# Writing VectorE's order over the output projection and twenty steps of the input projection, with weight sums a chunk sooner and results added by accumulating stores

## The chip, the cores and the metric

One core of a Trainium2 chip runs the whole program. The metric is device time in microseconds (us), the median of several executions; lower is better. "Chunk", "panel" and "step" are explained below.

## What is computed

One residual block on 512 tokens of width 2048, everything in float32 (cut to what matters; RMS norms, rotary angles and gains are left out):

```
h = rms_norm(x)
proj = h @ w_in                       # 2048 -> 15424 columns, split into 13 parts
o_conv = (b_gate * conv3(c_gate * u) * silu(conv_z)) @ w_conv_out
o_mla  = (attention(c_q, c_kv, k_rope) * silu(mla_z)) @ w_mla_out
o_mem  = (attention(mem_q, mem) * silu(mem_z)) @ w_mem_out
merged = sigmoid(g_conv)*o_conv + sigmoid(g_mla)*o_mla + sigmoid(g_mem)*o_mem
out = x + merged @ w_o
```

The change touches the first product (`w_in`) and the last line (`w_o`, and the sum with `x`).

## The kernel before

**Three products for one.** A float32 matrix is split into a high part and a low remainder, and a product is made as high*high + high*low + low*high, three TensorE matmuls (`mm3`, L161 to L163). The third is the first to read the low part of the weights. So for each piece of weights ScalarE writes the high part (`whi`, L281) and then VectorE the low part (`wlo`, L282).

**Panels and chunks.** `w_in`, `w_mla_out` and `w_o` go through a Strassen-like scheme: seven products in place of eight. A *panel* is 256 output columns and takes four *chunks* of weights, each 512 KB. A chunk is 42 matmuls (two blocks of rows, seven products, three matmuls). Before its split a chunk needs three *sums* on VectorE (L276, L277, L278), which fill the extra blocks of its `raw` tile. When a panel's last chunk is done, ScalarE copies one block out of PSUM (L317) and VectorE makes the panel's results in five instructions (L318, L323, L324, L326, L327), called the *eviction* here. The input projection has 60 panels, the output projection 8. Both begin with this order of chunks: three of panel 0, three of panel 1, then the last of panel 0 and the last of panel 1; after that panel by panel. In the texts c0, c1, ... are the chunks of the input projection and k0 to k31 those of the output projection, in this order; a *step* is one chunk.

**What prepares a chunk.** `queue` holds one entry for each chunk, and `begin(at, stage)` brings the entry at place `at` to a stage: 1 issues its load (SP's queue), 2 makes its sums, 3 its split. `take()` (L183) is called once a chunk, before TensorE's 42 matmuls: it splits this chunk (if need be) and the next, makes the sums of the one after that, issues the load of the third, runs one entry of the list `fills`, and pops the queue. There are four `raw` buffers, and two each for `whi` and `wlo`: ScalarE can write `whi` of chunk n+1 only when TensorE has finished chunk n-1.

**Who sets the order.** SP's and TensorE's instructions run in the order in which the code is written. For the other engines a scheduler picks the order, except inside `manual_dve`, where VectorE's is the written one too. In the kernel before, that stretch covers the end of the memory-key projection and the first 6 steps of the input projection (L821), and, later, the last product before the output projection and its first 9 steps (L1367 ff.).

**Other work of VectorE at these two places.** At the start of the input projection the last two of eight blocks of `x` are prepared through `fills`: a scaling and sums (L497, L255, L256, L258), then a split (L262). The first eight panels (`finish`) are kept as high and low parts: ScalarE squares them (L635, TensorE then adds the squares up, L641) and writes the high parts, VectorE the low ones (L134), and a store to DRAM goes through POOL. At the start of the output projection the last `merged` blocks get their sums (`sums_out`, L255 to L258, three instructions) and their split (`split_out`, L261 on ScalarE, L262 on VectorE), again through `fills`. Each panel of the output projection but the last is added to a block of `x` by VectorE (`result`, two instructions at L1350; the block `xr` was loaded by SP) and stored by ScalarE's queue. The last panel has a short way of its own (`tail_o`).

Of the kernel before, what the change touches and what calls it, by code (L numbers as in the profile page):

```python
# [30 lines left out]
P = 128  # L31
S = 512
# [75 lines left out]
def body(ctx, tc, a, out):  # L108
# [65 lines left out]
    def begin(at, stage):  # L174

        if at < len(queue):
            entry = queue[at]
            if len(entry) == 1:
                entry.append(entry[0]())
            while len(entry) < 2 + stage:  # L180
                entry.append(next(entry[1]))

    def take(ahead=1):  # L183
        for at in range(1 + ahead):
            begin(at, 3)
        begin(1 + ahead, 2)
        begin(2 + ahead, 1)
        if fills:
            fills.pop(0)()
        return queue.pop(0)[4]  # L190
# [332 lines left out]
    def staged_parts():  # L523
# [3 lines left out]
    upcoming(*plain_jobs([a["w_mem_kv"][grp][c] for grp in range(4) for c in range(8)], 512, True,  # L527
                         (staged_parts, None, None),
                         lambda c: memory_load(c + 1) if c < 4 else None))
    work = panels(xp, a["w_h"], len(SEQUENCE), lambda n: make(n), lambda n, e: finish(n, e), "aux")  # L530
    queue.insert(32 + 15, [lambda: rotary_weights()])
    parts_of_x = all_parts()
    manual_dve = ExitStack()
# [48 lines left out]
                nc.scalar.dma_start(mvdram[2 * (grp - 2) + i], t)  # L582
    for _ in parts_of_x:
        pass
    begin(2, 2)
    close_st()
    close_mt()
    pxb, close_xb = open_pool("xb", "right")
# [170 lines left out]

    conv_e = {}  # L760

    def make(n):
        return etile(), None

    angles = rotary()
# [50 lines left out]
    for i in (6, 7):  # L816
# [1 line left out]
        x_load(i, etile())  # L818
        steps = x_pair(i)
        fills += [lambda steps=steps: (next(steps), next(steps)), lambda steps=steps: next(steps)]  # L820
    for _ in range(6):  # L821
        next(work)
    manual_dve.close()
    for _ in work:
        pass
# [466 lines left out]
    def split_out(n):  # L1292
# [8 lines left out]
                 17: ((split_out, 1), (merged, 2), (merged, 3), (gate_load, 5), (gate_load, 6)),  # L1301
                 22: ((sums_out, 2),), 23: ((split_out, 2),), 24: ((sums_out, 3),),
                 25: ((split_out, 3), (merged, 4), (merged, 5), (gate_load, 7)),
                 29: ((sums_out, 4),), 30: ((split_out, 4), (merged, 6)), 31: ((sums_out, 5),),
                 32: ((split_out, 5),)}

    late_blocks = []
    for k in (6, 7):
# [6 lines left out]
    for tag, width in (("acc", 512), ("aux", 512), ("acc", 512), ("aux", 256), ("aux", 256)):  # L1315
        if done == 7:
            work = panels(xp, a["w_o"], 8, lambda n: make_o(n), lambda n, e: finish_o(n, e),
                          tail=lambda b, e: tail_o(b, e))
        banks = [bank(tag) for _ in range(width // P)]
        for n in dense_units(banks, width, actm, "F"):  # L1320
            if done == 0 and n == 8:
                for k in (6, 7):
                    nc.sync.dma_start(r32(late_blocks[k - 6]), amdram[k])
            if n % 4 == 3:
                step += 1
                for do, k in steps_out.get(step, ()):
                    do(k)
        for i in range(width // 256):
            gated(done + i, banks[2 * i:2 * i + 2])
        done += width // 256  # L1330
# [6 lines left out]

    def make_o(n):
        def middle():
            xrs[n] = pe.tile([P, 2, S], F32, tag="xr", name="xr", bufs=2)  # L1340
            nc.sync.dma_start(xrs[n].rearrange("p f n -> p (f n)"), a["xT"][:, n])
        return pe.tile([P, 8, H], F32, tag="e", name="e", bufs=2), middle

    def finish_o(n, e):
        fills.append(lambda: result(n, e))

    def result(n, e):
        xr = xrs[n]
        for f in range(2):
            vec.tensor_tensor(out=xr[:, f], in0=two(e)[:, f], in1=xr[:, f], op=ALU.add)  # L1350
            nc.scalar.dma_start(out[(2 * n + f) * P:(2 * n + f + 1) * P], xr[:, f])

    def tail_o(b, e):

# [10 lines left out]
        nc.sync.dma_start(out[15 * P:16 * P], xr[:, 1])  # L1365

    merged(7)  # L1367
    fills += [lambda: None, lambda: sums_out(6), lambda: split_out(6), lambda: sums_out(7), lambda: split_out(7)]
    for n, _ in enumerate(work):
        if n == 8:  # L1370
            manual_dve.close()
    close_e()
    close_m()
    close_x()
# [76 lines left out]
```

## Time and profile before

| | |
|---|---|
| median of 3 runs | 2164.0 us (2162.38 to 2164.59) |
| the profiled execution | 2162.43 us, of which its span is 2160.7 us |
| TensorE busy in the span | 2122.6 us (98%) |
| VectorE / ScalarE busy | 1728.2 us (80%) / 1010.8 us (47%) |
| input projection | about 107 to 1175 us of the span |
| output projection | about 1984 to 2157 us of the span |

In the timeline a row is: start, duration (both us), engine, line, operation, output<-inputs, shape, count, and in brackets the idle time before it with what ended it. Instructions of VectorE overlap a little, so the distance from one start to the next is what a place in its queue costs. Matmuls overlap too: one shows about 0.28 us, but they follow each other in 0.12 us. In the windows view a row is: the stretch, its length, then busy time and count of instructions of TensorE, its weight loads, VectorE, ScalarE and POOL, the granted TensorE clock (1.00 is full), the busy share of the DMA engines, and GB/s.

### The profile page before, as it was taken

How to read it: one execution, taken by the hardware profiler on the slowest of the kernel's cores; microseconds unless marked ns; L12 is line 12 of the kernel's file. 1: busy time of each engine (PE TensorE's matmuls, PEld its weight loads, DVE VectorE, ACT ScalarE, POOL GpSimd, SP SyncE). 2: the span in 40 equal slices, each digit the busy share in tenths (PEclk: the TensorE clock that was granted, in tenths of full speed). 3: DMA queues.
4: the chain of work that ended last, by engine and by line, in shares of the span. 5: the costliest groups of instructions: out<-in, count | busy, mean ns of one | idle time of the engine just before them, and what ended most of it. 6: DMA issues, size and time to landing. Idle time of an engine off the chain costs nothing.

```text
span 2160.7 us, 38707 instructions
## 1 busy us (share of the span) xinstructions
PE 2122.6 (98%) x16040; PEld 2037.7 (94%) x16040; DVE 1728.2 (80%) x2740; ACT 1010.8 (47%) x1235; POOL 130.9 (6%) x189
## 2 busy tenths in 40 slices
PE   9989999999999999999999999999999999999899
PEld 7889999999999999999999999898988899987899
DVE  5986878888888888888878876788886688856886
ACT  6743444444444344344444444777765533323333
POOL 0000000000000000000000000212111100011000
PEclk9999999999999999999999999999999999999999
DMA  8634443333333333343444336222346957667443
GB/s 330 248 98 137 158 135 128 128 127 128 127 127 127 125 125 126 126 136 133 137 137 142 131 129 241 90 104 81 112 158 245 355 203 208 201 213 199 141 162 107
DMA packets 93441, 338.51 MB, mean 157 GB/s; under 512 B 10896, under 2 KB 11152, under 8 KB 91216
## 3 DMA queue, kind: packets, MB, share of 16 engines
q1 hardware_dynamic: 70848, 252.58, 34.5%
q0 software_dynamic: 13920, 59.51, 8.6%
q10 hardware_dynamic: 8496, 23.94, 3.1%
q8 instruction: 125, 2.05, 0.4%
q14 instruction: 52, 0.43, 0.1%
HBM read 273.34 MB, written 62.65 MB: 156 GB/s over the span
## 4 chain that ended last, share of the span: by engine, by line
PE 84%; DVE 5%; ACT 2%; DMA 2%; issue 1%; POOL 0%; DVEq 0%; ACTq 0%; POOLq 0%
PE acc L161 14%; PE acc L163 14%; PE acc L162 14%; PE aux L161 13%; PE aux L163 13%; PE aux L162 13%; DVE wlo L282 2%; PE aux L363 1%; PE aux L997 1%; DMA raw<-in_w_h 1%; ACT whi L281 1%; DVE raw L276 0%; PE aux L977 0%; PE aux L980 0%; PE aux L978 0%
## 5 line engine op out<-in xcount | busy, mean ns | idle before, releaser
L281 ACT ACTIVATE whi<-raw 128x1792 fp32r<-128x1792 f32 x304 | 517.6, 1703 | 795.6 <-PE aux L162 336.7
L282 DVE TENSOR_TENSOR wlo<-raw,whi 128x1792 fp32r<-128x1792 f32 x304 | 614.8, 2022 | 204.2 <-ACT whi L281 203.5
L163 PE MATMUL aux<-xp,wlo 128*128 128x256 f32 (+1 forms) x1712 | 479.8, 280 | 6.3 <-DVE wlo L282 6.2
L161 PE MATMUL aux<-xp,whi 128*128 128x256 f32 (+1 forms) x1712 | 480.4, 281 | 0.0
L162 PE MATMUL aux<-xp,whi 128*128 128x256 f32 (+1 forms) x1712 | 479.2, 280 | 0.0
L163 PE MATMUL acc<-xp,wlo 128*128 128x256 f32 x1680 | 470.2, 280 | 3.4 <-DVE wlo L282 3.4
L161 PE MATMUL acc<-xp,whi 128*128 128x256 f32 x1680 | 470.8, 280 | 0.0
L162 PE MATMUL acc<-xp,whi 128*128 128x256 f32 x1680 | 469.6, 280 | 0.0
L163 PEld LDWEIGHTS aux<-xp,wlo 128*128 128x128 f32 (+1 forms) x1712 | 321.1, 188 | 7.5 <-DVE wlo L282 7.5
L161 PEld LDWEIGHTS aux<-xp,whi 128*128 128x128 f32 (+1 forms) x1712 | 320.6, 187 | 0.0
L163 PEld LDWEIGHTS acc<-xp,wlo 128*128 128x128 f32 x1680 | 316.0, 188 | 4.6 <-DVE wlo L282 4.6
L162 PEld LDWEIGHTS aux<-xp,whi 128*128 128x128 f32 (+1 forms) x1712 | 320.2, 187 | 0.0
L161 PEld LDWEIGHTS acc<-xp,whi 128*128 128x128 f32 x1680 | 315.6, 188 | 0.0
L162 PEld LDWEIGHTS acc<-xp,whi 128*128 128x128 f32 x1680 | 315.1, 188 | 0.0
L276 DVE TENSOR_TENSOR raw<-raw 128x512 f32<-128x512 f32 x304 | 208.3, 685 | 36.5 <-DMA raw<-in_w_h 31.8
L155 DVE TENSOR_TENSOR wlo<-raw,whi 128x1024 fp32r<-128x1024 f32 (+2 forms) x89 | 100.5, 1131 | 75.1 <-ACT whi L154 72.7
L154 ACT ACTIVATE whi<-raw 128x1024 fp32r<-128x1024 f32 (+2 forms) x89 | 87.7, 986 | 101.4 <-PE acc L162 43.3
L278 DVE TENSOR_TENSOR raw<-raw 128x256 f32<-128x256 f32 x304 | 127.9, 422 | 6.3
L277 DVE TENSOR_TENSOR raw<-raw 128x256 f32<-128x256 f32 x304 | 127.9, 422 | 5.7
L161 PE MATMUL acc<-whi,blk 128*128 128x384 f32 (+1 forms) x224 | 84.2, 376 | 0.0
L356 POOL TENSOR_TENSOR rs_r<-rs_t,mhalf 128x2 f32<-128x2 f32 (+2 forms) x71 | 65.2, 929 | 276.7 <-DVE rs_t L355 217.2
L163 PE MATMUL acc<-whi,blk 128*128 128x384 f32 (+1 forms) x224 | 80.9, 361 | 0.0
(360 smaller groups left out, 3896.7 us busy)
## 6 DMA issues: line engine op xcount, KB each, us to landing
raw<-in_w_h SPq DMA_DIRECT2D x240, 512.0 KB, 3.5
raw<-in_w_mla_out SPq DMA_DIRECT2D x32, 512.0 KB, 4.2
raw<-in_w_o SPq DMA_DIRECT2D x32, 512.0 KB, 3.6
raw<-in_w_mem_kv SPq DMA_DIRECT2D x31, 512.0 KB, 7.4
gdram<-e ACTq DMA_DIRECT2D x22, 512.0 KB, 2.9
raw<-in_w_ukv SPq DMA_DIRECT2D x16, 512.0 KB, 4.3
raw<-in_w_conv_out SPq DMA_DIRECT2D x16, 512.0 KB, 8.3
aadram<-z POOLq DMA_DIRECT2D x8, 896.0 KB, 3.9
```

The source lines that it names most:

```text
L154: act.activation(hi[:, cols], raw[:, cols], AF.Copy)
L155: vec.tensor_tensor(out=lo[:, cols], in0=raw[:, cols], in1=r32(hi[:, cols]), op=ALU.subtract)
L161: nc.tensor.matmul(o, lhsT=s[0], rhs=m[0], start=start, stop=False, skip_group_check=shared)
L162: nc.tensor.matmul(o, lhsT=s[0], rhs=m[1], start=False, stop=False, skip_group_check=shared)
L163: nc.tensor.matmul(o, lhsT=s[1], rhs=m[0], start=False, stop=stop, skip_group_check=shared)
L276: vec.tensor_tensor(out=f[:, 4:6], in0=f[:, 1:3], in1=f[:, 0:1].to_broadcast([P, 2, 256]), op=ALU.add)
L277: vec.tensor_tensor(out=f[:, 6], in0=f[:, 5], in1=f[:, 1], op=ALU.add)
L278: vec.tensor_tensor(out=f[:, 7], in0=f[:, 6], in1=f[:, 3], op=ALU.add)
L281: act.activation(hi, f[:, 1:8], AF.Copy)
L282: vec.tensor_tensor(out=lo, in0=f[:, 1:8], in1=r32(hi), op=ALU.subtract)
L356: pool.tensor_tensor(out=r, in0=t, in1=mhalf[:, :n], op=ALU.pow)
L363: nc.tensor.transpose(out=b[:, i * P:(i + 1) * P], in_=s, identity=ident)
```

## The change

1. **Sums a chunk sooner.** While the list `deeper` holds an entry, `take()` brings two chunks beyond the split ones to stage 2, and loads the one after. It is on from step 6 to step 19 of the input projection, and through all of the output projection.
2. **VectorE's order written.** The written stretch of the input projection grows from 6 steps to 20; that of the output projection now runs to its end.
3. **Results of the first five panels of the input projection** are finished one step later, through `fills`. At the end of the memory part the sums of c2 are no longer made ahead (`begin(2, 2)` became `begin(2, 1)`), and in the output projection the split of `merged` block 5 moved one place later.
4. **Results added by stores.** In panels 12 to 18 of the input projection SP issues seven copies of 512 KB from `xT` straight to `out` (DRAM to DRAM). In the output projection a panel's result is added to `out` by one accumulating store from POOL's queue. VectorE's 14 additions (L1350), the seven loads of `xr` and the 14 stores on ScalarE's queue are gone. The last panel stays as it was.

Core of the diff:

```diff
     def take(ahead=1):
         for at in range(1 + ahead):
             begin(at, 3)
-        begin(1 + ahead, 2)
-        begin(2 + ahead, 1)
+        more = 1 + ahead + len(deeper)
+        for at in range(1 + ahead, 1 + more):
+            begin(at, 2)
+        begin(1 + more, 1)
...
-    work = panels(xp, a["w_h"], len(SEQUENCE), lambda n: make(n), lambda n, e: finish(n, e), "aux")
+    work = panels(xp, a["w_h"], len(SEQUENCE), lambda n: make(n),
+                  lambda n, e: fills.append(lambda: finish(n, e)) if n < 5 else finish(n, e), "aux")
...
-    begin(2, 2)
+    begin(2, 1)
...
+    def out_rows(n):
+        return out[2 * n * P:2 * (n + 1) * P].rearrange("(f p) n -> p f n", f=2)
     def make(n):
+        if n >= 12 and n < 19:
+            nc.sync.dma_start(out_rows(n - 12), a["xT"][:, n - 12].rearrange("p (f n) -> p f n", f=2))
         return etile(), None
...
-    for _ in range(6):
+    for n in range(20):
+        if n == 6:
+            deeper.append(1)
         next(work)
+    deeper.clear()
     manual_dve.close()
...
     def finish_o(n, e):
-        fills.append(lambda: result(n, e))
-    def result(n, e):
-        xr = xrs[n]
-        for f in range(2):
-            vec.tensor_tensor(out=xr[:, f], in0=two(e)[:, f], in1=xr[:, f], op=ALU.add)
-            nc.scalar.dma_start(out[(2 * n + f) * P:(2 * n + f + 1) * P], xr[:, f])
+        nc.gpsimd.dma_start(out_rows(n), two(e), accum_op=ALU.add)
```

**Three places in VectorE's order.** Line numbers of the changed kernel are 4 or 5 higher for the same helper (L276 is L281, L282 is L287). First, the input projection from the split of the last block of `x` on. Before, c5 is `raw_1146`, c6 `raw_1208` and c8 `raw_1312`:

```order
L262 TENSOR_TENSOR xp7_1024<-e_1025,xp7_1024 128x1792
L276 TENSOR_TENSOR raw_1312<-raw_1312 128x512
L282 TENSOR_TENSOR wlo_1255<-raw_1146,whi_1254 128x1792
L276 TENSOR_TENSOR raw_1208<-raw_1208 128x512
L277 TENSOR_TENSOR raw_1312<-raw_1312 128x256
L277 TENSOR_TENSOR raw_1208<-raw_1208 128x256
L278 TENSOR_TENSOR raw_1312<-raw_1312 128x256
L278 TENSOR_TENSOR raw_1208<-raw_1208 128x256
L276 TENSOR_TENSOR raw_1364<-raw_1364 128x512
L277 TENSOR_TENSOR raw_1364<-raw_1364 128x256
L282 TENSOR_TENSOR wlo_1306<-raw_1208,whi_1305 128x1792
```

The same place after the change, with the same numbers for c5 and c6, and c7 as `raw_1261`:

```order
L267 TENSOR_TENSOR xp7_1021<-e_1022,xp7_1021 128x1792
L287 TENSOR_TENSOR wlo_1255<-raw_1146,whi_1254 128x1792
L281 TENSOR_TENSOR raw_1208<-raw_1208 128x512
L282 TENSOR_TENSOR raw_1208<-raw_1208 128x256
L283 TENSOR_TENSOR raw_1208<-raw_1208 128x256
L287 TENSOR_TENSOR wlo_1306<-raw_1208,whi_1305 128x1792
L281 TENSOR_TENSOR raw_1261<-raw_1261 128x512
```

Before, the sums of c8 and the first sums of c9 (`raw_1364`) stand ahead of the split of c6; now only c6's own sums stand between the splits of c5 and c6.

Second, a little later, from the split of c7 on. Before (c7 is `raw_1261`, c8 `raw_1312`):

```order
L282 TENSOR_TENSOR wlo_1358<-raw_1261,whi_1357 128x1792
L318 TENSOR_TENSOR e_1027<-aux_1029,e_1027 128x2x256
L278 TENSOR_TENSOR raw_1428<-raw_1428 128x256
L282 TENSOR_TENSOR wlo_1422<-raw_1312,whi_1421 128x1792
L323 TENSOR_TENSOR e_1027<-aux_1030,e_1027 128x512
```

After (c7 is `raw_1261`, c8 `raw_1312`, c9 `raw_1363`):

```order
L287 TENSOR_TENSOR wlo_1357<-raw_1261,whi_1356 128x1792
L281 TENSOR_TENSOR raw_1312<-raw_1312 128x512
L282 TENSOR_TENSOR raw_1312<-raw_1312 128x256
L283 TENSOR_TENSOR raw_1312<-raw_1312 128x256
L281 TENSOR_TENSOR raw_1363<-raw_1363 128x512
L282 TENSOR_TENSOR raw_1363<-raw_1363 128x256
L283 TENSOR_TENSOR raw_1363<-raw_1363 128x256
L323 TENSOR_TENSOR e_1024<-aux_1026,e_1024 128x2x256
L328 TENSOR_TENSOR e_1024<-aux_1027,e_1024 128x512
L329 SCALAR_TENSOR_TENSOR e_1024<-aux_1027,e_1024 128x256
L331 TENSOR_TENSOR e_1024<-aux_1028,e_1024 128x256
L332 TENSOR_TENSOR e_1024<-aux_1028,e_1024 128x256
```

The split of c8 follows directly on that. Before, it stood after the first instruction of panel 0's eviction; now two chunks' sums and the whole eviction stand between the splits of c7 and c8.

Third, the output projection from the split of k8 on. Before (k8 is `raw_22162`, k9 `raw_22213`, k11 `raw_22336`):

```order
L282 TENSOR_TENSOR wlo_22264<-raw_22162,whi_22263 128x1792
L276 TENSOR_TENSOR raw_22213<-raw_22213 128x512
L277 TENSOR_TENSOR raw_22336<-raw_22336 128x256
L277 TENSOR_TENSOR raw_22213<-raw_22213 128x256
L278 TENSOR_TENSOR raw_22336<-raw_22336 128x256
L278 TENSOR_TENSOR raw_22213<-raw_22213 128x256
L1350 TENSOR_TENSOR xr_21930<-e_21874,xr_21930 128x512 x2
L318 TENSOR_TENSOR e_22040<-aux_22042,e_22040 128x2x256
L323 TENSOR_TENSOR e_22040<-aux_22043,e_22040 128x512
L324 SCALAR_TENSOR_TENSOR e_22040<-aux_22043,e_22040 128x256
L326 TENSOR_TENSOR e_22040<-aux_22044,e_22040 128x256
L327 TENSOR_TENSOR e_22040<-aux_22044,e_22040 128x256
```

After (k8 is `raw_22116`, k9 `raw_22170`, k10 `raw_22221`):

```order
L287 TENSOR_TENSOR wlo_22273<-raw_22116,whi_22272 128x1792
L281 TENSOR_TENSOR raw_22221<-raw_22221 128x512
L282 TENSOR_TENSOR raw_22221<-raw_22221 128x256
L283 TENSOR_TENSOR raw_22221<-raw_22221 128x256
L323 TENSOR_TENSOR e_22050<-aux_22052,e_22050 128x2x256
L328 TENSOR_TENSOR e_22050<-aux_22053,e_22050 128x512
L329 SCALAR_TENSOR_TENSOR e_22050<-aux_22053,e_22050 128x256
L331 TENSOR_TENSOR e_22050<-aux_22054,e_22050 128x256
L332 TENSOR_TENSOR e_22050<-aux_22054,e_22050 128x256
L287 TENSOR_TENSOR wlo_22336<-raw_22170,whi_22335 128x1792
```

Before, the sums of k9 and k11 and the additions L1350 of panel 0 stand ahead of panel 1's eviction, and the split of k9 comes after it; now k9's sums are older, and between the splits of k8 and k9 stand only k10's sums and the eviction.

More of the change, by code (lines that the diff above doesn't have):

```diff
@@ L181, in begin @@
                 entry.append(next(entry[1]))
+    deeper = []
     def take(ahead=1):
@@ L1303, in body @@
                  25: ((split_out, 3), (merged, 4), (merged, 5), (gate_load, 7)),
-                 29: ((sums_out, 4),), 30: ((split_out, 4), (merged, 6)), 31: ((sums_out, 5),),
-                 32: ((split_out, 5),)}
+                 29: ((sums_out, 4),), 30: ((split_out, 4), (merged, 6)), 31: ((sums_out, 5),)}
     late_blocks = []
@@ L1318, in body @@
                           tail=lambda b, e: tail_o(b, e))
+            deeper.append(1)
         banks = [bank(tag) for _ in range(width // P)]
@@ L1339, in middle @@
         def middle():
-            xrs[n] = pe.tile([P, 2, S], F32, tag="xr", name="xr", bufs=2)
-            nc.sync.dma_start(xrs[n].rearrange("p f n -> p (f n)"), a["xT"][:, n])
+            if n == 7:
+                xrs[n] = pe.tile([P, 2, S], F32, tag="xr", name="xr", bufs=1)
+                nc.sync.dma_start(xrs[n].rearrange("p f n -> p (f n)"), a["xT"][:, n])
         return pe.tile([P, 8, H], F32, tag="e", name="e", bufs=2), middle
     def finish_o(n, e):
-        fills.append(lambda: result(n, e))
-    def result(n, e):
-        xr = xrs[n]
-        for f in range(2):
-            vec.tensor_tensor(out=xr[:, f], in0=two(e)[:, f], in1=xr[:, f], op=ALU.add)
-            nc.scalar.dma_start(out[(2 * n + f) * P:(2 * n + f + 1) * P], xr[:, f])
+        nc.gpsimd.dma_start(out_rows(n), two(e), accum_op=ALU.add)
     def tail_o(b, e):
@@ L1367, in body @@
     merged(7)
[L1368 to L1371, printed above, removed]
+    fills += [lambda: split_out(5), lambda: sums_out(6), lambda: split_out(6), lambda: sums_out(7), lambda: split_out(7)]
+    for _ in work:
+        pass
+    manual_dve.close()
     close_e()
```

## The prediction

> **What bounds the kernel now.** I read the engines' busy times first, then the windows view stage by stage, then the timeline of TensorE and of VectorE where TensorE loses time.
>
> ```profile
> PE 2122.6 (98%) x16040; PEld 2037.7 (94%) x16040; DVE 1728.2 (80%) x2740; ACT 1010.8 (47%) x1235; POOL 130.9 (6%) x189
> ```
>
> TensorE is the bound: it has 38 us of idle time in 2160.7. So this change can only win what TensorE loses in the two stages that it touches. The windows:
>
> ```profile
> 480.00:700.00 220.00, 220.00 (x1871) 220.00 (x1870) 187.15 (x254) 88.29 (x67) 1.60 (x3) 1.00 0.38 125
> ...
> 107.00:172.00 65.00, 55.17 (x453) 53.60 (x453) 57.35 (x77) 30.22 (x27) 0.73 (x1) 1.00 0.36 114
> ...
> 1984.00:2052.00 68.00, 57.10 (x461) 54.86 (x462) 60.18 (x78) 24.09 (x17) 1.41 (x2) 1.00 0.45 146
> 2052.00:2150.00 98.00, 98.00 (x835) 98.00 (x834) 80.57 (x108) 35.98 (x25) 0.00 (x0) 1.00 0.43 145
> ```
>
> In the middle of the input projection TensorE never rests: 220.00/1871 x 42 = 4.94 us a chunk. It idles in the first 65 us of that projection and the first 68 us of the output projection; from 2052 on it is full again. The rest of the kernel keeps its order. The first matmul that needs a chunk's low weights (L163) shows each chunk's delay:
>
> ```profile
> 107.12 0.39 PE L163 MATMUL aux<-xp,wlo 128*128 128x256 f32 x1
> ...
> 145.61 0.38 PE L163 MATMUL aux<-xp,wlo 128*128 128x256 f32 x1 [3.01 <-DVE wlo L282]
> ...
> 162.27 0.28 PE L163 MATMUL aux<-xp,wlo 128*128 128x256 f32 x1
> ...
> 166.98 1.84 PE L641 MATMUL acc<-one,e 128*128 128x1 f32 x16
> 169.76 1.95 PE L641 MATMUL acc<-one,e 128*128 128x1 f32 x16 [0.94 <-ACT e L635]
> ...
> 172.04 0.42 PE L163 MATMUL aux<-xp,wlo 128*128 128x256 f32 x1
> ```
>
> These are c0, c6, c9, two groups that add up squares, and c10. From c0 to c9 pass 55.15 us where nine chunks need 44.4: 10.7 us lost, all to late low weights. The 0.94 us ahead of the second group make 11.6.
>
> ```profile
> 1986.16 0.39 PE L163 MATMUL acc<-xo,wlo 128*128 128x256 f32 x1 [1.56 <-DVE wlo L282]
> 1992.75 0.39 PE L163 MATMUL acc<-xo,wlo 128*128 128x256 f32 x1 [1.37 <-DVE wlo L282]
> ...
> 2025.47 0.39 PE L163 MATMUL aux<-xo,wlo 128*128 128x256 f32 x1 [0.23 <-DVE wlo L282]
> 2032.64 0.39 PE L163 MATMUL acc<-xo,wlo 128*128 128x256 f32 x1 [1.96 <-DVE wlo L282]
> 2040.23 0.39 PE L163 MATMUL acc<-xo,wlo 128*128 128x256 f32 x1 [2.56 <-DVE wlo L282]
> 2047.38 0.39 PE L163 MATMUL acc<-xo,wlo 128*128 128x256 f32 x1 [1.93 <-DVE wlo L282]
> ```
>
> These are k0, k1, k7, k8, k9 and k10: 61.22 us for ten chunks that need 49.4, so 11.8 us lost. Why shows in VectorE's rows, and in one of ScalarE:
>
> ```profile
> 2001.57 2.03 DVE L282 TENSOR_TENSOR wlo<-raw,whi 128x1792 fp32r<-128x1792 f32 x1 [0.38 <-ACT whi L281]
> 2003.52 0.68 DVE L276 TENSOR_TENSOR raw<-raw 128x512 f32<-128x512 f32 x1
> ...
> 2005.04 2.02 DVE L262 TENSOR_TENSOR xo<-mg,xo 128x1792 fp32r<-128x1792 f32 x1
> 2007.03 2.03 DVE L282 TENSOR_TENSOR wlo<-raw,whi 128x1792 fp32r<-128x1792 f32 x1
> ```
> ```profile
> 2005.29 1.71 ACT L281 ACTIVATE whi<-raw 128x1792 fp32r<-128x1792 f32 x1 [2.16 <-DVE raw L278]
> ```
>
> A split costs VectorE 1.95 us, a chunk's sums 1.52 (2003.52 to 2005.04), a block's split 1.95. The high weights start when the sums of the same chunk end. So split, sums, high weights (1.71 and some 0.2 of gaps), split is a chain, and it turns in 5.46 us (2001.57 to 2007.03) where TensorE needs 4.94.
>
> **Output projection, part by part.** With its sums a chunk older, `whi` waits only for TensorE to release the buffer, and VectorE's own work sets the pace. From k2 to k6, two chunks hold two splits, two chunks' sums, one set of block sums and one block split: 2 x 1.95 + 2 x 1.52 + 1.52 + 1.95 = 10.4 us against 9.9 of TensorE, so 0.5 us are lost for each pair, 1.2 in all with the odd chunk. k0 depends on the same VectorE work as before (I get its L163 at 1985.95). The split of k1 follows on one split, one chunk's sums and the two gate products, and ends before TensorE wants it: the 1.65 us lost there go. For k7 VectorE is ahead. Then come the evictions and the additions:
>
> ```profile
> 2034.45 1.28 DVE L1350 TENSOR_TENSOR xr<-e,xr 128x512 f32<-128x512 f32 x2
> 2035.65 0.68 DVE L318 TENSOR_TENSOR e<-aux,e 128x512 f32<-128x512 f32 x1
> ...
> 2038.16 2.01 DVE L282 TENSOR_TENSOR wlo<-raw,whi 128x1792 fp32r<-128x1792 f32 x1
> ```
>
> An eviction is 2.51 us, a panel's additions 1.2. Before, k8, k9 and k10 lost 2.2, 2.65 and 2.2 us to them and to sums of later chunks put ahead. After, k8's split has room; k9's follows a split, sums and the eviction, 1.95 + 1.52 + 2.51 = 5.98, and is late by about 0.7; k10 is free. Loss after the change 1.2 + 0.7 = 1.9 in place of 11.8, and 0.2 at k0: a gain of 10.1. From k11 on no loss is seen before; after, the eviction stands ahead of the split in the written order, with some 0.25 us to spare, so I count 0. The additions of later panels were hidden anyway. The tail after the last matmul keeps its instructions.
>
> **Input projection.** The rows for the block of `x`, the low parts, and the wait that goes:
>
> ```profile
> 115.08 1.23 DVE L497 TENSOR_TENSOR e<-e,xscale 128x1024 f32<-128x1024 f32 x1 [1.10 <-ACT e L496]
> ...
> 117.88 2.02 DVE L282 TENSOR_TENSOR wlo<-raw,whi 128x1792 fp32r<-128x1792 f32 x1
> ...
> 142.47 0.69 DVE L276 TENSOR_TENSOR raw<-raw 128x512 f32<-128x512 f32 x1 [3.01 <-DMA raw<-in_w_h]
> ...
> 171.81 1.41 DVE L134 SCALAR_TENSOR_TENSOR e<-e,gains 128x512 fp32r<-128x512 f32 x2
> 173.13 0.42 DVE L277 TENSOR_TENSOR raw<-raw 128x256 f32<-128x256 f32 x1
> ```
>
> Scaling and sums of a block of `x` take 2.80 us, the low parts of a panel 1.32. I walk along the splits in the written order. c1's now stands ahead of c2's sums and starts at 110.4 (1.5 sooner). Each next one is later by 1.95 + 1.52 and what stands between: block sums (c2, c4): 6.27; block split (c3, c5): 5.42; nothing but the wait for `whi` of the same chunk (c6, c7): 5.25; a second chunk's sums and an eviction (c8): 7.5; low parts and an eviction (c9): 7.3. That gives 116.7, 122.1, 128.4, 133.8, 139.05, 144.3, 151.8 and 159.1 for c2 to c9. L163 follows a split's start by 2.08, so c9's is at 161.2, and with 4.94 and two groups of 1.84 c10's is at 169.8 in place of 172.04: a gain of 2.2. It is small because the deeper sums (1.52) and the whole evictions now stand ahead of c8 and c9, which lose 2.5 and 2.4, while c6, which lost 3.1 to sums of c9 waiting for their load, loses 0.3. Finishing panels 0 and 1 a step later still gives ScalarE their squares by 160.2, ahead of the two groups at 166, so the 0.94 us wait goes. After c10 VectorE has caught up, and order and slack are those of a full TensorE.
>
> A chunk's sums now follow two splits, not three, behind the one that frees its buffer: 9.9 us for a load. **Stores and copies:**
>
> ```profile
> raw<-in_w_h SPq DMA_DIRECT2D x32, 512.0 KB, 3.4
> ```
> ```profile
> L1243 POOL DMA_DIRECT2D mgdram<-sg x8: 862/871/904, 1778.3 to 1899.7; - x8
> ...
> DMA to landing us min/median/max: 2.3/5.8/10.0
> ```
> ```profile
> 380.98 2.02 DVE L282 TENSOR_TENSOR wlo<-raw,whi 128x1792 fp32r<-128x1792 f32 x1 [1.35 <-ACT whi L281]
> ...
> 397.77 0.68 DVE L276 TENSOR_TENSOR raw<-raw 128x512 f32<-128x512 f32 x1
> ```
>
> A load lands in 3.4 us: covered. The accumulating stores have twins in the attention output projection (POOL 0.87 us each, landing at most 10.0), and the `e` buffer that one holds is wanted a panel (19.8 us) later; behind a store that waits for its eviction stand only the next stores on POOL: 0. ScalarE's 14 store issues and SP's seven loads of `xr` go unseen, since ScalarE is busy for only 24.09 of the 68 us. No row shows a copy from DRAM to DRAM. It stands on SP's queue ahead of a load. That load is issued when a split ends (383.0) and its sums come at 397.77, so with 3.4 for the load a copy may take 11.3 us unseen. Nearest is the accumulating store, 5.8 and at most 10.0: cost 0; below nothing isn't possible, since those loads are on time; the other end is a rival.
>
> Sum: 10.1 + 2.2 = 12.3 off the profiled 2162.43 gives 2150.1. The median is 1.6 higher, so 2164.0 - 12.3 = **2151.7 us**.
>
> **One clock row to weigh.**
>
> ```profile
> 170.00:174.00 4.00, 4.00 (x28) 4.00 (x28) 3.62 (x7) 0.93 (x2) 0.47 (x1) 0.71 0.39 131
> 174.00:178.00 4.00, 4.00 (x31) 4.00 (x31) 1.03 (x2) 0.00 (x0) 0.07 (x1) 0.86 0.66 266
> ```
>
> Behind the two groups of small matmuls and their wait the granted clock falls to 0.71 and 0.86, which costs 4 x 0.29 + 4 x 0.14 = 1.7 us. The groups stay, so the sum leaves this as it is. [...]
>
> **Rivals.** (1) The clock stays up: 1.7 us more, 2150.0. For it, the wait that goes; against it, 3.7 us of small matmuls remain. (2) The input projection gives nothing: c8 and c9 lose what c6 wins, if evictions find ScalarE's copies or parts later by 1 us each: 2164.0 - 10.1 = 2153.9. (3) The accumulating stores hold VectorE up: each of 7 stands 0.87 us in VectorE's way and only 0.25 is spare, so 7 x 0.62 = 4.3: 2156.0. The split at 1778.75, under such a store, took its usual 2.03:
>
> ```profile
> 1778.75 2.03 DVE L282 TENSOR_TENSOR wlo<-raw,whi 128x1792 fp32r<-128x1792 f32 x1 [0.40 <-ACT whi L281]
> ```
>
> [...] (4) Slower: the copies take over 11.3 us and hold up the weights behind them. At twice the slowest accumulating store, 20 us, seven cost 7 x 8.7 = 61 and the time is 2164.0 - 12.3 + 61 = 2213; it decides from 13 us a copy on. For it, both sides are in DRAM; against it, the DMA engines are busy only 0.38 there. (5) No change: the stalls return as waits of another engine, 2162 to 2164; ScalarE at 47% speaks against it.
>
> **How the numbers follow.** Chances: forecast 0.56, (1) 0.09, (2) 0.20, (3) 0.05, (4) 0.05, (5) 0.05. A measurement of this kernel can tell 0.2%, 4.3 us, from no change. Faster by more: forecast and (1) to (3), 0.90; same: (5), 0.05; slower: (4), 0.05. The range holds forecast, (1), (2) and most of (3). Down, to (1) I add 3 us for some twenty distances of 0.15 us each: 2147; up, (2) and (3) together, 2158.
>
> **What would show it.** Right: L163 of k10 some 61 - 10 = 51 us behind k0's; c6 without a wait over 0.5 us; c8 and c9 with waits near 2 us each; c10 about 62.7 us behind c0; `whi` in the output projection waiting for TensorE. Wrong: waits of VectorE for loads between 370 and 520 us (4), splits longer than 2.03 under POOL's stores (3), or lost time from k11 on.

## The result, and the profile after

The changed kernel takes 2151.0 us (median of 4 runs, 2149.23 to 2151.8) beside 2164.3 us (median of 4 runs) for the kernel before; the ratio is 0.9935, with a 95% interval of 0.9921 to 0.9950. The forecast was 2151.7 us. The profiled execution took 2150.61 us, of which its span is 2148.8.

The windows of the two stages, as they were read before the change:

```profile
107.00:172.00 65.00, 57.98 (x463) 56.01 (x462) 59.49 (x75) 30.90 (x28) 1.40 (x3) 0.97 0.38 130
1984.00:2052.00 68.00, 67.53 (x562) 67.05 (x563) 62.86 (x82) 27.68 (x19) 5.00 (x5) 0.97 0.51 137
2052.00:2140.00 88.00, 88.00 (x749) 88.00 (x748) 68.61 (x86) 30.64 (x22) 4.71 (x4) 1.00 0.46 123
```

In the first 68 us of the output projection TensorE is now busy for 67.53 us (57.10 before) and runs 562 matmuls (461 before). In the first 65 us of the input projection it runs only 10 more than before, and the granted clock of both stretches has fallen from 1.00 to 0.97. The prediction did not foresee that clock.

The timeline's rows of TensorE for c0, c6, c8, c9, the two square groups (now one row) and c10; and for k0, k9 and k10:

```profile
107.91 0.39 PE L163 MATMUL aux<-xp,wlo 128*128 128x256 f32 x1 [0.76 <-DVE wlo L287]
...
142.09 0.39 PE L163 MATMUL aux<-xp,wlo 128*128 128x256 f32 x1 [0.24 <-DVE wlo L287]
...
155.04 0.58 PE L163 MATMUL aux<-xp,wlo 128*128 128x256 f32 x1 [2.28 <-DVE wlo L287]
...
162.34 0.39 PE L163 MATMUL aux<-xp,wlo 128*128 128x256 f32 x1 [0.66 <-DVE wlo L287]
...
167.15 3.63 PE L648 MATMUL acc<-one,e 128*128 128x1 f32 x32
...
170.96 0.28 PE L163 MATMUL aux<-xp,wlo 128*128 128x256 f32 x1
...
1983.88 0.38 PE L163 MATMUL acc<-xo,wlo 128*128 128x256 f32 x1 [1.86 <-DVE wlo L287]
...
2030.24 0.38 PE L163 MATMUL acc<-xo,wlo 128*128 128x256 f32 x1 [0.30 <-DVE wlo L287]
...
2035.30 0.28 PE L163 MATMUL acc<-xo,wlo 128*128 128x256 f32 x1
```

Output projection: from k0 to k10 pass 51.42 us (61.22 before). Input projection: from c0 to c10 pass 63.05 us (64.92 before), but c0 itself comes 0.79 us later, and c8's wait of 2.28 us is new. That the chain through the high weights is broken shows in VectorE's rows and in ScalarE's:

```profile
2002.40 2.02 DVE L287 TENSOR_TENSOR wlo<-raw,whi 128x1792 fp32r<-128x1792 f32 x1
...
2007.38 2.02 DVE L287 TENSOR_TENSOR wlo<-raw,whi 128x1792 fp32r<-128x1792 f32 x1
```
```profile
2004.56 1.71 ACT L286 ACTIVATE whi<-raw 128x1792 fp32r<-128x1792 f32 x1 [3.05 <-PE aux L162]
```

The distance of these two splits is 4.98 us (5.46 between the splits at 2001.57 and 2007.03 before), though a chunk's sums and a block's sums stand between them. The high weights wait for TensorE, no longer for the chunk's own sums.

**The clock.** In three of the rows below of the changed kernel, and in one of the kernel before, the granted clock is 0.50 over 3.41 or 3.42 us; I call such a stretch a slow-clock window. The windows view, first of the kernel before and then of the changed one:

```profile
140.97:144.38 3.41, 1.64 (x15) 1.44 (x13) 1.87 (x3) 0.36 (x1) 0.00 (x0) 1.00 0.02 7
144.38:147.80 3.42, 2.19 (x18) 2.19 (x19) 2.88 (x5) 0.34 (x1) 0.00 (x0) 1.00 0.36 110
...
168.27:171.68 3.41, 2.47 (x22) 2.39 (x23) 2.82 (x4) 2.66 (x4) 0.00 (x0) 1.00 0.28 111
171.68:175.09 3.41, 3.41 (x18) 3.41 (x18) 2.70 (x7) 0.00 (x0) 0.54 (x1) 0.50 0.64 228
```
```profile
151.66:155.07 3.41, 1.13 (x11) 0.92 (x9) 3.38 (x6) 2.58 (x4) 0.00 (x0) 1.00 0.00 0
155.07:158.49 3.42, 3.42 (x16) 3.42 (x17) 3.29 (x6) 1.56 (x2) 0.34 (x1) 0.50 0.52 158
...
168.72:172.13 3.41, 3.41 (x31) 3.41 (x31) 3.10 (x4) 0.21 (x1) 0.00 (x0) 1.00 0.62 197
172.13:175.55 3.42, 3.42 (x19) 3.42 (x18) 0.52 (x3) 0.00 (x0) 0.00 (x0) 0.50 0.42 153
...
1981.20:1984.61 3.41, 1.54 (x11) 1.26 (x10) 3.34 (x5) 2.97 (x2) 0.00 (x0) 1.00 0.48 192
1984.61:1988.02 3.41, 3.41 (x19) 3.41 (x18) 3.38 (x5) 0.32 (x1) 0.87 (x1) 0.50 0.47 156
```

Before, c6's wait of 3.01 us (its end is at 145.61) had no slow-clock window behind it: the clock is 1.00 to 171.68. The only one in these stages stood behind the square groups (at 171.68). After the change it is still there (at 172.13), and two more have come: one behind c8's wait of 2.28 us, one behind k0's of 1.86.

**Stores and copies.** The rows of `out`:

```profile
L775 SPq DMA_DIRECT2D out<-in_xT x7: 584/590/723, 373.2 to 491.9; - x7
L1363 POOL DMA_DIRECT2D out<-e x7: 1172/1181/1220, 2022.6 to 2127.4; - x7
```

A copy lands in 4.4 to 5.8 us (median 5.1). An accumulating store takes POOL 1.18 us, where the row used for its price was 0.87.

### The profile page after: what moved, and what is told of

Its sections match the earlier page's. It is cut to its first block, busy times and chain, and to the rows that moved or that the text cites. A ratio compares the mean times of both kernels' runs of the same rounds, so it can differ in the third digit from the quotient of the medians.

```text
span 2148.8 us, 38695 instructions
## 1 busy us (share of the span) xinstructions
PE 2123.0 (99%) x16040; PEld 2040.0 (95%) x16040; DVE 1723.3 (80%) x2726; ACT 1011.4 (47%) x1235; POOL 139.1 (6%) x196
## 4 chain that ended last, share of the span: by engine, by line
PE 89%; DVE 7%; ACT 2%; issue 1%; DMA 1%; POOL 0%; SPq 0%; DVEq 0%; ACTq 0%; POOLq 0%
PE acc L161 15%; PE acc L163 15%; PE acc L162 15%; PE aux L161 13%; PE aux L163 13%; PE aux L162 13%; DVE wlo L287 2%; PE aux L368 1%; PE aux L1013 1%; DVE raw L281 1%; ACT whi L286 1%; PE aux L993 0%; DVE raw L282 0%; PE acc L648 0%; PE aux L996 0%
## 5 line engine op out<-in xcount | busy, mean ns | idle before, releaser
L287 DVE TENSOR_TENSOR wlo<-raw,whi 128x1792 fp32r<-128x1792 f32 x304 | 614.9, 2023 | 205.9 <-ACT whi L286 205.2
L281 DVE TENSOR_TENSOR raw<-raw 128x512 f32<-128x512 f32 x304 | 208.5, 686 | 23.0 <-DMA raw<-in_w_h 19.4
L283 DVE TENSOR_TENSOR raw<-raw 128x256 f32<-128x256 f32 x304 | 128.5, 423 | 7.0
L282 DVE TENSOR_TENSOR raw<-raw 128x256 f32<-128x256 f32 x304 | 128.4, 422 | 6.5
```

Of the source, the lines that this page charges most:

```text
L281: vec.tensor_tensor(out=f[:, 4:6], in0=f[:, 1:3], in1=f[:, 0:1].to_broadcast([P, 2, 256]), op=ALU.add)
L282: vec.tensor_tensor(out=f[:, 6], in0=f[:, 5], in1=f[:, 1], op=ALU.add)
L283: vec.tensor_tensor(out=f[:, 7], in0=f[:, 6], in1=f[:, 3], op=ALU.add)
L287: vec.tensor_tensor(out=lo, in0=f[:, 1:8], in1=r32(hi), op=ALU.subtract)
```

## The experiments

The theory, called A in the expectations: the sums a chunk sooner break the chain in the output projection, and that is nearly the whole gain; the written order and the stores keep it; the input projection gives a little. Each kernel is given by its edit against the changed kernel, the last two by theirs against the kernel ahead of them. The kernel before was run beside them: medians 2162.15 us (first four kernels), 2163.34 (next four), 2162.64 (next two) and 2163.63 (last).

### The output part alone

```diff
-    begin(2, 1)
+    begin(2, 2)
...
-                  lambda n, e: fills.append(lambda: finish(n, e)) if n < 5 else finish(n, e), "aux")
+                  lambda n, e: finish(n, e), "aux")
...
-    for n in range(20):
-        if n == 6:
-            deeper.append(1)
+    for n in range(6):
         next(work)
-    deeper.clear()
```

> The output projection as changed (deeper sums, written order, accumulating stores, with the seven copies), the input projection's order, depth and finishing as before. Theory A (the sum of the prediction): the output projection alone brings about 10.1 us, so about 2154, and L163 of k10 stands about 51.4 us behind that of k0 as in the changed kernel. Rival B (the input part brings more than its rows show, since the changed kernel is also 1.3 us earlier at places between the two): about 2157 or more. Rival C (the copies cost something that the input part's gain hides): over 2155, with waits of VectorE for loads between 370 and 520 us.

Measured: 2153.56 us (5 runs), ratio 0.9951 [0.9935, 0.9966]. c0 to c10 take 64.78 us, as before the change; k0 to k10 take 51.97. The output part alone brings most of the gain: its ratio lies within the noise of the changed kernel's, which was 0.9935 above and 0.9949 in the second comparison below.

### The input part alone

The written stretch, the depth of the sums and the later finishing of the input projection stay; the output projection, its additions and the split of `merged` block 5 are as before, and there are no copies.

> The input projection's order, depth and finishing as changed, everything else as before (no copies, results added by VectorE, scheduler's order from the tenth step of the output projection on). Theory A: c0 to c10 takes 63.0 us in place of 64.9 and the kernel is 1 to 2.5 us faster than before: 2162 to 2163.5. Rival B: 5 us or more faster, below 2159.5. Both: two slow-clock windows in the first 180 us of the span, as in the changed kernel, since the wait of 2.3 us at c8 stays.

Measured: 2162.50 us (10 runs), ratio 0.9995 [0.9986, 1.0004]. The input part alone gains nothing that can be measured. c0 to c10 take 64.45 us, though c0 to c9 take 54.42 in place of 55.15. What c9 wins goes between c9 and c10 (10.03 us; 8.62 in the changed kernel), where two slow-clock windows now stand at the square groups: the groups take 4.78 us (3.63 in the changed kernel), and the matmuls behind them stand 0.21 us apart until 175.5. The old output projection shows more of them behind its waits, at k8 and at k10 (0.50 from 2046.12 to 2049.53). At k0 this kernel is 1.6 us ahead of the one before; at the last chunk it is level with it. The rows at k8:

```profile
2029.05:2032.46 3.41, 1.54 (x13) 1.54 (x14) 3.41 (x6) 0.00 (x0) 0.00 (x0) 1.00 0.00 0
2032.46:2035.87 3.41, 3.41 (x19) 3.41 (x18) 3.27 (x8) 1.70 (x1) 0.00 (x0) 0.50 0.41 154
```

### The output projection without the deeper sums

```diff
                           tail=lambda b, e: tail_o(b, e))
-            deeper.append(1)
```

> The changed kernel without the deeper sums in the output projection: written order and stores stay. Theory A (the chain split, sums, high weights, split sets the pace, and only older sums break it): the written order puts each chunk's sums right behind the split before, so every chunk from k1 on turns in 5.46 us in place of 4.94: about 30 x 0.52 = 15.6 us more, less the 1.9 us that the changed kernel loses there itself: about 2165, slower than the kernel before or level with it. Rival D (the written order is what helps, the scheduler's early sums of later chunks were the harm): 2151 to 2154, chunks of 5.46 us up to k7 only.

Measured: 2169.82 us (5 runs), ratio 1.0029 [1.0016, 1.0043]: the change without this one line is slower than the kernel before. The waits view of this kernel from 1972 us on, and two splits late in the stage:

```profile
ACT whi L286 <- DVE raw L283: 105.5, 29, 4.3
```
```profile
2079.11 2.02 DVE L287 TENSOR_TENSOR wlo<-raw,whi 128x1792 fp32r<-128x1792 f32 x1
...
2084.55 2.03 DVE L287 TENSOR_TENSOR wlo<-raw,whi 128x1792 fp32r<-128x1792 f32 x1 [1.90 <-ACT whi L286]
```

In the changed kernel that wait for L283 comes to 5.5 us in all. The chain turns in 5.44 us (2079.11 to 2084.55), and in 5.98 where an eviction stands in it, to the last chunk, because the order is now written to the end; the scheduler of the kernel before had left the chain after k10. Theory A gave about 2165; it had not counted the evictions in the chain, seven times 0.5 us. So the depth is what pays, and without it the written order is a loss here. The rival that gave the order itself the gain fell.

### The results added by VectorE, without copies and accumulating stores

The additions (L1350 before), the loads of `xr` and the stores on ScalarE's queue come back through `fills`, in the written order; the seven copies go.

> The changed kernel with the results of the output projection added by VectorE and stored by ScalarE's queue as before (loads of xr again, no copies); order written, sums deeper. Theory A: only the addition of panel 0, 1.2 us, stands on the path, between the splits of k8 and k9; later ones fit: 1 to 1.5 us more, about 2152.2. Rival E (VectorE's load is the bound there and the removed 14 additions are a large part of the gain): 5 us or more slower than the changed kernel, 2156 or above.

Measured: 2154.77 us (4 runs), ratio 0.9961 [0.9946, 0.9975]. The additions stand in front of k9's eviction and split:

```profile
2024.29 2.02 DVE L287 TENSOR_TENSOR wlo<-raw,whi 128x1792 fp32r<-128x1792 f32 x1
2027.74 1.29 DVE L1363 TENSOR_TENSOR xr<-e,xr 128x512 f32<-128x512 f32 x2
...
2031.46 2.01 DVE L287 TENSOR_TENSOR wlo<-raw,whi 128x1792 fp32r<-128x1792 f32 x1
```

The distance is 7.17 us (5.97 in the changed kernel): 1.2 more, the price of a panel's additions. Later panels have slack for most of that. In the stage as a whole this kernel gains 8.5 us, the changed one 9.6 to 10.4 (worked out below), so the stores and copies together are worth 1 to 2 us by the profiles; the ratios' intervals overlap.

### VectorE's order in the output projection written for nine steps only

```diff
-    for _ in work:
-        pass
-    manual_dve.close()
+    for n, _ in enumerate(work):
+        if n == 8:
+            manual_dve.close()
```

> The changed kernel with VectorE's order in the output projection written for its first 9 steps alone, as before; the deeper sums and the accumulating stores stay. Theory A (the depth of the sums brings the gain there, the written order past step 9 only keeps what it brings): evictions spread out by the scheduler may put sums of later chunks ahead of a split once a panel, 0 to 1 us for some of six panels, 2151 to 2155. Rival J (the order past step 9 is a part of the gain of its own, as in the kernel before, where k9 and k10 lost 2.65 and 2.2 us): 2155 to 2160, with waits of TensorE for the low weights of 2 us or more at k9 to k12.

Measured: 2156.23 us (10 runs), ratio 0.9968 [0.9956, 0.9980]. Here my theory was wrong, and rival J right: the order past step 9 is a part of the gain of its own, some 5 us. VectorE's rows where k9's split should stand:

```profile
2031.41 0.69 DVE L281 TENSOR_TENSOR raw<-raw 128x512 f32<-128x512 f32 x1 [2.60 <-DMA raw<-in_w_o]
...
2033.02 2.01 DVE L287 TENSOR_TENSOR wlo<-raw,whi 128x1792 fp32r<-128x1792 f32 x1
```

The scheduler puts the first sums of a later chunk into the middle of an eviction; their load has not landed, and VectorE waits 2.60 us with k9's split behind it. TensorE waits 3.8 us at k9, two slow-clock windows follow (0.50 from 2033.52 to 2040.35), and from k8 to k10 pass 16.3 us in place of 10.5. From k10 on the chunks follow each other in 4.95 us, as in the changed kernel: all of the loss is made at this one place.

### The input projection without the deeper sums

```diff
-        if n == 6:
-            deeper.append(1)
         next(work)
```

> The changed kernel without the deeper sums in the input projection; its 20 steps stay written, and the output projection stays as it is. Theory A (written order alone keeps the chain split, sums, high weights, split at 5.45 us a chunk): the steps from c6 on lose 0.5 us each as long as VectorE's order is the written one, 14 x 0.5 = 7 us less what c8 and c9 no longer lose to the sums of a further chunk (2.3 and 0.7), so 3 to 5 us slower than the changed kernel: 2154 to 2156. Rival H (the stretch is too short to matter, and TensorE's loss at c8 was made by the deeper sums alone): 2148 to 2151.

Measured: 2152.95 us (4 runs, 2151.17 to 2156.26), ratio 0.9952 [0.9933, 0.9971]. The median lies between the two expectations, and the runs cover both. Up to c10 the rival is right: c8 waits 0.94 us in place of 2.28, since the deeper sums no longer stand ahead of its split, no slow-clock window follows (1.00 to 171.16), and c0 to c10 take 61.52 us, less than in the changed kernel. Later it loses 2.3 us between 243 and 265 us: TensorE waits 1.85 us at 244.57 for a split that stands behind an eviction, and 0.46 us at 261.93 for one that stands behind sums whose load VectorE had waited for. What the two come to over many executions is too small to tell here.

### The seven copies in one row

```diff
-        if n >= 12 and n < 19:
-            nc.sync.dma_start(out_rows(n - 12), a["xT"][:, n - 12].rearrange("p (f n) -> p f n", f=2))
+        if n == 12:
+            for k in range(7):
+                nc.sync.dma_start(out_rows(k), a["xT"][:, k].rearrange("p (f n) -> p f n", f=2))
```

> The changed kernel with all seven copies of x to the output issued in one row ahead of panel 12 of the input projection, in place of one a panel. Two theories of what a copy costs. Theory F (a copy takes the loads' DMA engines for its own 3 to 10 us, and the 11.3 us that a load can be late by are what hides it): seven in a row hold one weight load up by 20 us or more, so TensorE loses 10 to 40 us once, near 373 us of the span, VectorE's waits for loads there grow from 0.7 us to at least 8, and the whole takes 2161 us or more. Rival G (transfers of a queue share the DMA engines, which are busy only 0.38 there, so a load behind copies is hardly later): no wait of TensorE near 373 us, 2150 to 2152 us.

Measured: 2151.36 us, one run. The waits from 360 to 520 us, and the issues:

```profile
DVE raw L281 <- DMA raw<-in_w_h: 4.5, 4, 1.6
```
```profile
out<-in_xT SPq DMA_DIRECT2D x7, 512.0 KB, 11.9
```

The time is that of rival G, but the waits lie between the two theories. Each copy lands 8.0 to 13.0 us after its issue (median 11.9), the last one 18.6 us after the first was issued, and VectorE's waits for loads rise from 0.7 us in all to 4.5; TensorE loses 2.9 us, once (the start of the same chunk's high weights moves by that between 398 and 407 us). So even in a row they cost 2.9 us in this profile, and one a panel is far from that.

### The deeper sums two steps sooner, and the first panels later still

```diff
+    def finish_later(n, e):
+        if n == 0:
+            fills.append(lambda: None)
+        fills.append(lambda: finish(n, e))
...
-        if n == 6:
+        if n == 4:
             deeper.append(1)
```

`finish_later` takes the place of the one-step delay for the same five panels.

> The changed kernel with two edits in the input projection: the deeper sums from step 4 (not 6) on, and the finishing of its first panels one further step later. In the changed kernel VectorE idles at c6 and c7 (it waits for the high weights) and is then late at c8 by 2.28 us and at c9 by 0.66. Theory A (only the order of VectorE's work makes the loss at c8): the sums of c7 fall into that idle time, the splits of c5 to c9 take about 21.8 us in place of 25.7, c10 comes 2 to 4 us earlier behind c0, TensorE shows no wait over 1 us at c8, and the slow-clock window behind that wait (some 1.5 us) goes as well: 2147 to 2149 us against 2151.0. Rival B (the time is given back by the clock: another wait sets off another slow window, as in the kernel that had the input part alone): c10 earlier, the whole the same, 2150 to 2152. Rival C (the sums pulled forward wait for their loads): VectorE shows waits for loads of over 1 us between c4 and c7, c10 no earlier, 2151 to 2154.

Measured: 2153.43 us (6 runs), ratio 0.9954 [0.9937, 0.9970]. In the input projection theory A holds: c8 has no wait, c9 one of 0.28 us, and by 240 us the kernel is 3.2 us ahead of the one before. At 1351 us all of it and more is lost (TensorE waits 3.9 us for a load). SP's rows there, the wait between them, and the store that it waits for:

```profile
1317.08 2.23 SPq L870 DMA_DIRECT2D blk<-latdram  x4
...
1339.05 0.79 SPq L870 DMA_DIRECT2D blk<-latdram  x2
```
```profile
SPq L870 <- DMA gdram<-e: 19.5, 1, 19.5
```
```profile
1334.47 0.53 POOL L824 DMA_DIRECT2D gdram<-e  x1 [12.25 <-ACT e L823]
```

In the changed kernel the same six loads issue within 3.28 us. By the waits that the loads carry, the last two now go into memory that the last gate panel's `e` buffer leaves, and the order in which `e` buffers come free at the start of the projection decides which buffer that is.

### The same with another buffer in that place, beside the changed kernel again

```diff
-                  lambda n, e: finish_later(n, e) if n < 5 else finish(n, e), "aux")
+                  lambda n, e: finish_later(n, e) if n < 3 else finish(n, e), "aux")
```

> The kernel with sums from step 4 on and later finishing gained 3.7 us of TensorE in the input projection and lost 6.3 us at 1351 us: there two loads of the latents stood on SP's queue until 1339.05, when the last gate panel's store had landed, since the e buffer of that panel lies where those two tiles go. Which e buffer lies where hangs on the order in which buffers of e come free at the start of the input projection. This kernel finishes only three panels later (with the one further step), which changes two places in VectorE's order, and by the waits that its loads carry those two latents no longer stand behind that store. Theory A (the buffer alone made the loss): the six loads of latents issue within 5 us, no wait of TensorE for them, c10 some 3 to 4 us earlier than in the changed kernel, and the whole is 2147 to 2149 us. Rival B (the gain is given back elsewhere anyway, by slow-clock windows): 2150 to 2153.

> The changed kernel once more, on the same chip as the one beside it. Every theory expects 2150 to 2152 us, and slow-clock windows near 153 us of the span; whether the one near 1983 us shows again tells whether it belongs to the kernel or to the execution.

Measured: 2152.55 us (6 runs, 2145.98 to 2153.17), ratio 0.9942 [0.9928, 0.9956], and for the changed kernel on the same chip 2151.55 us (5 runs), ratio 0.9949 [0.9937, 0.9960]. The six loads issue within 4.21 us and nothing is lost at 1351 us, so the wait for that store was the cause there. Yet the whole is no faster. The windows of the kernel with the edit, and VectorE's rows ahead of the wait that lies in the last two of them:

```profile
163.66:167.07 3.41, 3.41 (x18) 3.41 (x18) 3.41 (x4) 0.51 (x1) 0.56 (x1) 0.50 0.61 233
167.07:170.48 3.41, 3.41 (x18) 3.41 (x18) 1.46 (x5) 0.00 (x0) 0.00 (x0) 0.50 0.97 346
...
214.86:218.27 3.41, 0.79 (x7) 0.58 (x5) 2.60 (x3) 2.59 (x3) 0.53 (x1) 1.00 0.09 38
218.27:221.68 3.41, 3.04 (x14) 3.05 (x15) 3.34 (x5) 0.00 (x0) 0.00 (x0) 0.50 1.00 360
```
```profile
214.34 0.75 DVE L134 SCALAR_TENSOR_TENSOR e<-e,gains 128x512 fp32r<-128x512 f32 x1 [0.46 <-ACT e L130]
215.90 0.75 DVE L134 SCALAR_TENSOR_TENSOR e<-e,gains 128x512 fp32r<-128x512 f32 x1 [0.81 <-ACT e L130]
216.56 2.02 DVE L287 TENSOR_TENSOR wlo<-raw,whi 128x1792 fp32r<-128x1792 f32 x1
```

c10 comes 6.3 us earlier than before (165.74). Two slow-clock windows stand at the square groups, where the kernel before has one, and at c12 5.5 us are left. Then TensorE waits 2.99 us at 218.64; that wait and the slow window behind it take 4.6 us, and a slow window behind the next square group (0.50 from 228.51 to 231.92) takes 1.5. The time is that of rival B, but the largest loss is not the clock's. By the count of the matmuls the chunk that waits is c17, inside the written stretch (the expectation for the next kernel calls it c20, the first one behind it). Its split stands behind panel 3's eviction and behind the low parts of panel 3 (L134), which wait for ScalarE: 8.73 us after the split of c16. In the changed kernel, where panels 3 and 4 are finished a step later too, it is 5.96 us. So the edit that moved the buffer brought this wait in.

The changed kernel's second profile has k0 to k10 in 52.02 us, with a slow-clock window behind k0 again (no row of it is printed here). That does not make it the kernel's own: the kernel with the copies in one row has the same output projection and the same wait of 1.86 us at k0, and the granted clock stayed at 1.00 behind it, from 1984.47 to 2049.32 us. At the start the same wait of c8 had another end:

```profile
152.41:155.82 3.41, 1.88 (x16) 1.88 (x17) 3.34 (x5) 3.13 (x5) 0.00 (x0) 1.00 0.27 71
155.82:159.23 3.41, 3.33 (x29) 3.13 (x27) 3.27 (x8) 0.00 (x0) 0.76 (x1) 1.00 0.50 203
159.23:162.64 3.41, 1.40 (x11) 1.40 (x12) 3.34 (x5) 3.29 (x4) 0.00 (x0) 1.00 0.60 221
162.64:166.06 3.42, 3.42 (x19) 3.42 (x18) 3.42 (x5) 0.59 (x1) 0.57 (x1) 0.50 0.50 201
```

c8's 2.27 us had no slow-clock window behind it (1.00 from 152.41 to 162.64 us); c9's 2.09 us had one (0.50 from 162.64 to 166.06), right ahead of the groups, where TensorE is the bound. c0 to c10 took 64.32 us.

### Twenty-eight written steps

```diff
-    for n in range(20):
+    for n in range(28):
```

(against the last kernel)

> The last kernel gained 5.5 us up to c10 and gave 6 back by 234 us: TensorE waited 2.99 us for the low weights of c20, the first chunk after the written stretch, where the scheduler puts an eviction and two low parts ahead of the split, and slow-clock windows followed. This kernel is the same with 28 written steps in place of 20, so that the split of c20 stands ahead again. Theory A (handover of VectorE's order made the loss): no wait of TensorE over 1 us between c10 and c30, one slow-clock window less, 2148 to 2150 us. Rival B (the small matmuls of the square groups, which now come with less idle time ahead of them, set off slow windows whatever the order): the windows behind the groups stay at two or three, and the whole is 2150 to 2153 us. A third way: a written order holds VectorE up at the end of the longer stretch, 2153 us or more.

Measured: 2158.28 us (12 runs), ratio 0.9977 [0.9963, 0.9992]. Theory A fell: TensorE waits 2.98 us at 218.95 as in the last kernel, waits 2.40 us again at 246.41 and at 270.66, and by then has lost 5 us more. The third way came true, and VectorE's rows show how: each of the three splits stands directly behind the low parts of a panel that is not finished later (panels 3, 4 and 5). The written order holds the split up, not the handover.

## Why the prediction was right, and where not

**The output projection: mechanism and size right.** Forecast 10.1 us. Taken at the start of the same chunk's high weights, the gain from 1972 us to the last chunk is 10.4 us in the profiled execution, 9.6 in the second one and 9.4 with the output part alone. The kernel without the deeper sums shows that the broken chain is the cause. Its parts: k1's wait is gone; from k11 on every chunk takes 4.94 to 4.95 us; k9 waits 0.30 to 0.65 us (0.7 forecast). The 1.2 us that VectorE should cost from k2 to k6 are hardly seen as waits, because the slow-clock window behind k0 takes some 1.6 us from TensorE there (sixteen matmuls 0.22 us apart, 0.12 behind it) and lets VectorE run ahead. In the kernel with another buffer the stage goes as it was summed: k0 to k10 in 51.25 us, with small waits at k4, k6 and k9.

**The input projection: the walk right, its gain lost behind it.** The splits of c2 to c9 stand at the distances forecast within 0.2 us, and c8 waits 2.28 us (2.5 forecast). c10 should come 62.7 us behind c0; it came 63.05 us behind in one execution and 64.32 in the other, where a slow window stands ahead of the square groups and none behind them. At c12, past both places, the two agree. The rows of c12's high weights, of before, of the changed kernel and of its second profile (those of c0 start at 103.30, 104.09 and 103.01):

```profile
178.26 1.70 ACT L281 ACTIVATE whi<-raw 128x1792 fp32r<-128x1792 f32 x1 [7.33 <-issue]
```
```profile
177.32 1.70 ACT L286 ACTIVATE whi<-raw 128x1792 fp32r<-128x1792 f32 x1 [8.39 <-PE aux L162]
```
```profile
176.24 1.70 ACT L286 ACTIVATE whi<-raw 128x1792 fp32r<-128x1792 f32 x1 [6.87 <-PE aux L162]
```

Counted from c0, both are 1.7 us earlier than before, of 2.2 forecast. Ten chunks later almost nothing is left; the same three rows for c22:

```profile
243.04 1.71 ACT L281 ACTIVATE whi<-raw 128x1792 fp32r<-128x1792 f32 x1 [1.07 <-PE acc L162]
```
```profile
242.63 1.70 ACT L286 ACTIVATE whi<-raw 128x1792 fp32r<-128x1792 f32 x1 [3.24 <-PE acc L162]
```
```profile
243.04 1.70 ACT L286 ACTIVATE whi<-raw 128x1792 fp32r<-128x1792 f32 x1 [3.24 <-PE acc L162]
```

So 0.4 and 0.0 us. In the first profile c0 itself came 0.79 us later than before (not in the second, so the order alone does not make it). In both, c17 loses 0.5 us: in the written order its split stands behind its neighbour's sums and panel 3's eviction, 5.96 us after the split of c16. In the second, 1.5 us more go between c12 and c22 (66.80 us between their rows above, 65.31 in the first). Two steps of the prediction failed here. "After c10 VectorE has caught up" was wrong by the 0.5 us at c17. And "the groups stay, so the sum leaves this as it is" took the clock as one fixed loss behind the groups. Other profiles have this order of the input projection's sums, splits and evictions too. In the changed kernel's two and in the one with nine written steps in the output projection one slow window stands at the first square groups, as before (at 172.13, 162.64 and 173.26 us), and the gain at c12, counted from c0, is 1.73 to 1.75 us. With the input part alone and with the results added by VectorE two stand there (the groups take 4.78 and 4.85 us, 3.63 in the changed kernel), and it is 0.1 to 0.3 us. The result is that of rival (2), not for its reason; where the clock made it, it is rival (1) with its sign turned: the clock did not stay up, it fell more often.

**The sum came out right all the same**, and that is luck: the 2.2 us missed in the input projection were made up by gains that were not forecast. In the kernel before, TensorE waited 0.65 us for low weights at 1177.57 us, and that wait is gone in both profiles (0.9 us with what follows). k0 comes 2.28 us earlier in the first profile: 1.1 us of that is there by 1950 us, 0.7 comes in the last product ahead of it, and 0.5 at k0 itself (0.2 forecast). I forecast neither that wait nor the first two of these, and no run here singles out their cause.

**Stores and copies: right.** VectorE waits 0.7 us for loads from 370 to 520 us, splits under POOL's stores take 2.02 us (the one at 2022.20 beside the store at 2022.6), and seven copies in a row cost 2.9 us once. The store's price on POOL was low, 0.87 us for 1.18, and nothing waited for it. Rivals (3) and (4) fell.

**What was missing in the reasons.** The theory above held that the written order past step 9 only keeps the gain; it is worth some 5 us, by the one choice that the scheduler makes at k9.

## What to carry to other kernels

Where two engines hand work to each other in a ring, look for the step whose input is made on the same engine just before it: making that input one turn sooner (here one line of code) was worth more than 15 us in the output projection against the same order without it. There, the order written by hand paid only with such slack in it. The end of a written stretch is a place where the scheduler can put work ahead that waits for a load; and a written order keeps a bad place too, as the low parts of panel 3 ahead of a split did. A wait of 2 us on the bound engine was not priced here by its length alone: look whether the granted clock falls behind it, as it did behind k0's 1.86 us (0.50 for 3.41 us) and not behind c6's 3.01 in the kernel before.

## What the runs showed of the hardware that was not expected

In these runs a longer wait of TensorE did not make it surer that the granted clock fell behind it:

| kernel | wait of TensorE | granted clock from its end on |
|---|---|---|
| before | 3.01 us at c6 | 1.00 to 171.68 us |
| changed, first profile | 2.28 us at c8 | 0.50 from 155.07 to 158.49 |
| changed, second profile | 2.27 us at c8 | 1.00 to 162.64 |
| changed, second profile | 2.09 us at c9 | 0.50 from 162.64 to 166.06 |
| changed, first profile | 1.86 us at k0 | 0.50 from 1984.61 to 1988.02 |
| copies in one row | 1.86 us at k0 | 1.00 to 2049.32 |
| nine written steps in the output projection | 3.8 us at k9 | 0.50 to 2040.35 |
| another buffer | 2.99 us at c17 | 0.50 to 221.68 |

So between two executions of the changed kernel the same wait of c8 had a slow-clock window behind it in one and none in the other. What decides it these rows do not show.

What such a window took differs too. Behind k0, where TensorE is the bound, it was some 1.6 us, an estimate from sixteen matmuls 0.22 us apart in place of 0.12. Behind c8 in the first profile, where VectorE sets the pace, c9's wait shrank from the 2.09 us of the second to 0.66.
